# A hybrid decoder step: where the samples' cached keys are turned and multiplied, and how eight PSUM banks are shared out

## The chip, the cores and the metric

The kernel runs on one core of a Trainium2 chip. The metric is the device time of one execution in microseconds (us). A core has TensorE (PE, matrix multiply into PSUM), VectorE (DVE), ScalarE (ACT), GpSimd (POOL) and SyncE (SP), which here issues nearly all DMAs. Each engine works through a list of its own in order; semaphores hold an instruction until what it needs is there. PSUM has eight banks of 512 float32 values in each of 128 partitions.

## The reference

One step of a model with two layers, on a prompt of 2048 tokens and on 8 samples of 4 tokens each, whose past of 2048 tokens lies in a paged cache. The even layer has two branches behind one input projection: a gated recurrence (HGRN2), and "forgetting" attention. The odd layer is a gated recurrence (GLA). What the change touches is the attention of the samples:

```
def fox_sample(q, k, v, log_f, k_pages, v_pages, logf_pages, page_table):
    db, T, H, dh = q.shape                                   # 8, 4, 4, 128
    k_past = k_pages[page_table].reshape(db, -1, H, dh)      # 16 pages of 128 rows for each sample
    v_past = v_pages[page_table].reshape(db, -1, H, dh)
    lf_past = logf_pages[page_table].reshape(db, -1, H)
    suffix_past = (lax.cumsum(lf_past, axis=1, reverse=True) - lf_past).swapaxes(1, 2)
    logit_past = jnp.einsum('bthd,bshd->bhts', q, k_past) * scale + cum_new[..., None] + suffix_past[:, :, None, :]
    ...
    p = jax.nn.softmax(jnp.concatenate([logit_past, logit_new], axis=-1), axis=-1)
    return jnp.einsum('bhts,bshd->bthd', p[..., :P], v_past) + jnp.einsum('bhts,bshd->bthd', p[..., P:], v)
```

The prompt's attention (`fox_prompt`) is causal softmax attention with the same forget bias over the 2048 tokens, 4 heads of 128.

## The kernel before

The kernel has three stages, written one behind the other: `phase_even` (the even layer's projections and its recurrence), `phase_fox` (attention) and `phase_odd` (the even layer's output projection, and the odd layer). A scheduler orders each engine's instructions by their place in the program and by times that it simulates; `issue_after(x)` puts what a block issues behind instruction x on x's engine. Float32 accuracy in the wide matmuls comes from three float16 matmuls (`mm3`, lines 630 to 632).

**The even layer.** The tokens are treated in two halves (hf 0 with the samples' 32 rows, hf 1). Each half has 16 dense units of 256 columns, so units 0 to 15 and 16 to 31 by one count; one unit of the second half is 8 row blocks x 8 k tiles x 3 matmuls. A unit yields after each group of matmuls, in the second half four times (n = 0 to 3). `staged` (line 1267) runs a unit and beside it fetches, measures, scales and splits the weights of units to come; in the second half the split weights are read back from DRAM (`kept_unit`). `mux` lays a head's recurrence (`lin_attn`) beside two or three units. The PSUM banks here are "pj" 3 (projections), "gr" 2 (recurrence, transposes), "st" 1 and "o" 2.

**What runs beside the units.** `beside` (line 1147) loads and measures, from unit 16 on, one after another of the 20 weight units of later layers (`later_unit`; 1 MB each, buffer "lr"), to have their scale ready. `ahead` (line 1537) prepares cached keys. A key group is four pages, one of each of four samples: 1 MB, and there are 32 groups. In 20 units (`AHEAD`) one group is read into `kp` (four DMAs, line 1531), turned by four transposes of 32x32 blocks on DVE into `kt` (`turn_block`, line 1535), and written to the DRAM tensor `kT` (line 1551). Load stands at n = 1, three turns at n = 3, the fourth at n = 0 of the next unit, and the store at its n = 1.

**The attention stage.** `until` (line 97) lays two generators beside each other by costs that are written into their yields. `fox_prompt` works through 16 groups (head, 512 query rows): scores into PSUM banks "s" (2 of them), bias and maximum on DVE (line 1421), exponential on ACT (1429), scaling on POOL (1437), transposes on PE into banks "t" (1457), split on ACT and DVE (1464, 1465), and the product with the values into bank "o". `fox_sample` first goes through the 32 key groups: 20 are read back turned from `kT` (`turned`, line 1591), 12 are read and turned here (`pages`, `turn`). Each group is multiplied with the samples' queries by 16 small matmuls (`score`, line 1697; columns of the array in four strips of 32, `strips` gives them priority over the program's order) into bank "sc". `qz` holds the queries with zeros where a page belongs to another sample. The forget bias (`past`: an indirect gather of log forget values, four transposes, a few matmuls; bank "kt", 2 of them) is added by 64 more small matmuls, then come the softmax, four groups of transposes of the probabilities, and 34 groups of matmuls with the value pages (line 1777).

Of the kernel before, what the change touches and what calls it, by code (L numbers as in the profile page):

```python
# [28 lines left out]
NH = 4  # L29
# [5 lines left out]
SC_C = 1350.0  # L35
# [4 lines left out]
EWR = 3  # L40
# [10 lines left out]
AHEAD = (*range(4, 14), *range(19, 29))  # L51
PRE = len(AHEAD)
TURNED = [n for n in range(2 * 16) if (n + 1) * PRE // 32 > n * PRE // 32]
PAST = 3
VAHEAD = 3
KAHEAD = 6
PKLAG = 4
# [10 lines left out]
PV_C = 5860.0  # L68
# [60 lines left out]
class Kern:  # L129
# [6 lines left out]
    def consts(self):  # L136
# [31 lines left out]
        self.kT = dp.tile([PRE, P, 4 * 512], F32, name="kT")  # L168
# [465 lines left out]
    def proj_fm(self, pps, act, W, off, M, hf, evac, nm):  # L634
        for c0, n in self.segs(hf):
            ps = pps.tile([P, 512], F32, tag="pj", name=f"pf_{nm}{c0}")
            for k in range(KT):
                self.mm3(ps[:M, :n], [x[:, k, off : off + M] for x in W],
                         [x[:, k, c0 : c0 + n] for x in act], k == 0, k == KT - 1)
            evac(ps[:M, :n], c0, n)  # L640
            yield 24 * (n / 2.4 + 3)

    def proj_tm(self, pps, act, W, hf, evac, nm, width=256, pairs=True, banks=("pj",)):
# [3 lines left out]
        for g in range(0, len(tl), per):  # L647
# [8 lines left out]
            for j, (c0, n) in enumerate(grp):  # L656
                for k in range(KT):
                    self.mm3(ps[:n, j], [x[:, k, c0 : c0 + n] for x in act],
                             [x[:, k, :width] for x in W], k == 0, k == KT - 1)
# [463 lines left out]
    def phase_even(self):  # L1123
# [4 lines left out]
        with pool("act", side="right") as ap, pool("w", side="right") as w0, pool("wl", side="right") as wp1, \  # L1128
                pool("wk") as wp0, pool("nrm") as n0, pool("stt") as sp, pool("ps", space=PSUM) as pp0:
            wpool = self.wpool = Pool(w0, {"w": 3, "wr": EWR, "rm": 2, "pow": 2, "lr": 2})  # L1130
            wp = Pool(wp0, {"c4": 7, "sam": 1, "v4": 3, "sg": 3, "pd": 1, "kt": 2, "y": EY, "xpad": 1, "vs": 3,
                            "ss": 2, "rs_t": 2, "rs_r": 2}, Pool(wp1, {"c2": EC2, "th": ETH}))
# [22 lines left out]
            self.later, self.kept = [], {}  # L1155
# [4 lines left out]
            for hf in range(2):  # L1160
# [7 lines left out]
                def dense(a, b, hf=hf):  # L1168
                    return self.staged(us, 16 * hf + a, 16 * hf + b, beside)
# [33 lines left out]
                else:  # L1203
                    self.sx_odd = self.gain_scale(self.g_odd, pps, "pj", "o")
                    self.later = [self.later_unit(wpool, pps, w, cols, key, undo) for w, cols, key, undo in
                                  self.later_units()]
# [7 lines left out]
                drain(dense(2 - hf, 3))  # L1214
                drain(mux(lin(0), LIN_E[hf], dense(3, 5), 2 * cost))
# [35 lines left out]
            for n in range(2):  # L1251
                self.ahead(wpool, 32, n)
# [14 lines left out]
    def staged(self, us, a, b, beside=None):  # L1267
# [15 lines left out]
        for j in range(a, b):  # L1283
# [8 lines left out]
            for n, c in enumerate(us[j][1](self.ready.pop(j))):  # L1292
                for x in todo.pop(0) if todo else ():
                    step(*x)
                if beside:
                    self.ahead(self.wpool, j, n)
                    if n in (1, 3):
                        beside(2 * j + n // 2)
# [54 lines left out]
    def phase_fox(self):  # L1353
# [17 lines left out]
    def fox_prompt(self, fx, pps, caus):  # L1371
# [4 lines left out]
        self.sample_done, self.last_exp, self.pks = False, None, []  # L1376
# [23 lines left out]
        def scores(h, G, b):  # L1400
# [7 lines left out]
            for j in range(G + 1):  # L1408
                w = 512 if j < G else (b + 1) * P
                ps = pps.tile([P, 512], F32, tag="s", name=f"s{h}{tb}{j}")  # L1410
                with ExitStack() as st:
                    if len(self.pks) > PKLAG:
                        st.enter_context(self.tc.issue_after(self.pks[-1 - PKLAG].ins))
                    self.last_pe = self.mm3(ps[:, :w], q, [x[:, :w] for x in K[h, j]], True, True)
# [122 lines left out]
    def ahead(self, pool, u, n):  # L1537
# [3 lines left out]
        m, old = (AHEAD.index(x) if x in AHEAD else None for x in (u, u - 1))  # L1541

        def turns(xs):
            with self.tc.issue_after(self.last_dve.ins):
                for x in xs:
                    self.turn_block(self.kt_ahead, self.kp_ahead, x)

        if n == 0 and old is not None:
            turns([3])
        if n == 1 and old is not None:  # L1550
            nc.sync.dma_start(self.kT[old], self.kt_ahead.rearrange("p a s -> p (a s)"))
        if m is None:
            return
        tag = "lr" if u < 16 else "wr"
        if n == 1:
            self.kp_ahead = pool.tile([P, 4, 512], F32, tag=tag, name=f"kp{m}")
            with self.tc.issue_after(self.last_sp.ins):
                regs = self.page_regs(TURNED[m] % 2, TURNED[m] // 2)
                for x in range(4):
                    self.page_load(self.kp_ahead, "cache_fox_k", regs[x], x)  # L1560
        if n == 3:
            self.kt_ahead = pool.tile([P, NH * 4, P], F32, tag=tag, name=f"kt{m}")
            turns(range(3))

    def fox_sample(self, fs, pps):
# [25 lines left out]
        def turned(n):  # L1591

            kt = fs.tile([P, NH * 4, P], F32, tag="pg", name=f"ktd{n}")
            with ExitStack() as st:
                if len(asked) < 8:
                    st.enter_context(self.tc.issue_after(first_v.ins))
                d = nc.sync.dma_start(kt.rearrange("p a s -> p (a s)"), self.kT[n])
            asked.extend([d] * 4)
            kts.append((kt, [d]))

        yield S0
        marks, steps, first_v = [], [], self.last_vload
# [13 lines left out]
        qz = one([P, 2, NH * 4, TS], "qz")  # L1616
# [672 lines left out]
```

## Time and profile before

| | |
|---|---|
| median of 3 runs | 2319.26 us (2313.12 to 2326.04) |
| the profiled execution | 2321.78 us, its span 2320.1 us |
| mean granted TensorE clock | 0.983 |
| PE busy | 2206.3 us, 95% of the span |
| DVE, ACT, POOL busy | 1399.2, 991.6, 727.1 us |
| DMA | 403.87 MB, mean 174 GB/s |
| even layer, second half | about 480 to 882 us of the span |
| attention stage | about 882 to 1262 us |

A row of the profile's groups names the line, the engine and the operation, what is written from what, the shape and the count; then come the busy time in us and the mean ns of one, then the engine's idle time just ahead of these instructions and who ended it. In tables by stretch each engine has its busy us and its count of instructions; then come the mean granted TensorE clock (1.00 is full), the share of time in which the 16 DMA engines were busy, and GB/s. Rows of instructions in order of time give the start, the length and, in brackets, the idle time ahead and its releaser. PEld is the loading of PE's stationary operand.

### The profile page before, as it was taken

The page shows a single profiled execution, that of the slowest core. Times are in us where ns is not written, and L with a number is a line of the kernel's source. Part 1 is how long each engine was busy: PE and PEld are TensorE (multiplying, and loading weights), DVE is VectorE, ACT ScalarE, POOL GpSimd, SP SyncE. Part 2 cuts the span into 40 slices and gives each one's busy share as a digit, 9 for nine tenths or more (in the row PEclk, how much of TensorE's full clock was granted, in tenths as well). Part 3 has the DMA queues.
Part 4 walks back from the last instruction along what each step waited for, and adds up shares of the span by engine and source line. Part 5 has one row for each costly group of instructions (what it writes and reads, how often), then busy time and mean ns, then how long its engine had stood idle before and what let it go on. Part 6 is the DMA issues. An engine that isn't in the chain of part 4 may idle for free.

```text
span 2320.1 us, 58035 instructions
## 1 busy us (share of the span) xinstructions
PE 2206.3 (95%) x23316; PEld 1580.6 (68%) x23316; DVE 1399.2 (60%) x3138; ACT 991.6 (43%) x2200; POOL 727.1 (31%) x788
## 2 busy tenths in 40 slices
PE   7999999999999996889999999999999999999998
PEld 5677667864655684556446888677677666667887
DVE  7766567626555555768768445366665655547554
ACT  6433344221121223446566443555544545545343
POOL 2223334001111103434346245154452432323232
PEclk9999999999999998999999999999999999999999
DMA  6356665975766549997984969524224431115553
GB/s 203 121 163 187 192 194 188 284 177 172 224 197 183 169 136 271 250 264 271 277 265 142 311 196 262 126 75 146 73 92 97 126 94 58 47 58 165 169 188 151
DMA packets 365296, 403.87 MB, mean 174 GB/s; under 512 B 108529, under 2 KB 303410, under 8 KB 355810
## 3 DMA queue, kind: packets, MB, share of 16 engines
q1 hardware_dynamic: 362882, 393.54, 57.4%
q0 software_dynamic: 2144, 6.62, 0.8%
q8 instruction: 183, 3.00, 0.5%
q14 instruction: 87, 0.71, 0.1%
HBM read 265.77 MB, written 117.39 MB: 165 GB/s over the span
## 4 chain that ended last, share of the span: by engine, by line
PE 69%; DMA 10%; DVE 8%; ACT 4%; issue 4%; SPq 2%; POOL 2%; POOLq 0%; DVEq 0%; ACTq 0%
PE pt_o L630 4%; PE pt_o L631 4%; PE pt_o L632 4%; DMA pgcache_fox_k<-in_cache_fox_k 3%; PE pt_Cv L630 2%; PE pt_Cv L632 2%; PE pt_Cv L631 2%; PE pt L1457 2%; DMA ny<-in_x_prompt 1%; PE pv L1777 1%; PE gl_A L761 1%; PE o_C L914 1%; PE pt_Av L632 1%; PE pt_Av L630 1%; PE pt_Av L631 1%
## 5 line engine op out<-in xcount | busy, mean ns | idle before, releaser
L630 PE MATMUL pt_o<-w_o,act 128*128 128x256 f16 x1024 | 278.9, 273 | 1.3 <-ACT sg1C L687 1.3
L631 PE MATMUL pt_o<-w_o,act 128*128 128x256 f16 x1024 | 278.9, 273 | 0.0
L632 PE MATMUL pt_o<-w_o,act 128*128 128x256 f16 x1024 | 278.7, 273 | 0.0
L630 PEld LDWEIGHTS <-act 128*128 128x128 f16 x2304 | 226.6, 98 | 37.1 <-issue 3.7
L631 PEld LDWEIGHTS <-act 128*128 128x128 f16 x2304 | 226.7, 98 | 33.5 <-issue 4.8
L632 PEld LDWEIGHTS <-act 128*128 128x128 f16 x2304 | 226.6, 98 | 30.7 <-issue 2.2
L794 POOL TENSOR_TENSOR kA<-kA,fA 128x512 f32<-128x512 f32 (+1 forms) x56 | 76.8, 1372 | 338.8 <-PE gl_A L761 275.7
L1429 ACT ACTIVATE L<-L,nm,kc 128x512 f32<-128x512 f32 (+3 forms) x160 | 118.2, 741 | 75.1 <-DVE nm L1427 58.6
L630 PE MATMUL pt_Cv<-w_Cv,act 128*128 128x256 f16 (+1 forms) x512 | 141.4, 276 | 0.3 <-DMA act<-xs 0.3
L632 PE MATMUL pt_Cv<-w_Cv,act 128*128 128x256 f16 (+1 forms) x512 | 141.3, 276 | 0.0
L631 PE MATMUL pt_Cv<-w_Cv,act 128*128 128x256 f16 (+1 forms) x512 | 141.3, 276 | 0.0
L1437 POOL TENSOR_SCALAR L<-L,nm 128x512 f32<-128x512 f32 (+3 forms) x160 | 100.0, 639 | 130.7 <-DVE nm L1433 65.4
L794 POOL TENSOR_TENSOR kC<-kC,fC 128x512 f32<-128x512 f32 (+1 forms) x56 | 81.9, 1463 | 136.3 <-PE gl_C L761 91.4
L1464 ACT ACTIVATE th<-pt 128x512 f16<-128x512 f32 (+3 forms) x159 | 81.0, 527 | 94.6 <-PE pt L1457 92.7
L1465 DVE TENSOR_TENSOR tl<-pt,th 128x512 f16<-128x512 f32 (+3 forms) x159 | 94.5, 605 | 13.0 <-ACT th L1464 11.2
L1457 PE MATMUL pt<-ident,L 128*128 128x128 f32 x544 | 89.6, 280 | 9.4 <-DVE tl L1465 7.5
L1457 PEld LDWEIGHTS pt<-ident,L 128*128 128x128 f32 x544 | 65.5, 143 | 36.1 <-DVE tl L1465 12.8
L793 DVE TENSOR_TENSOR qC<-qC,fC 128x512 f32<-128x512 f32 (+1 forms) x56 | 72.9, 1301 | 21.1 <-PE gl_C L761 21.1
L1977 ACT ACTIVATE vC<-pt_Cv,kc 128x512 f32<-128x512 f32 (+1 forms) x40 | 23.9, 598 | 133.9 <-PE pt_Cv L632 133.9
L630 PE MATMUL s<-k,q 128*128 128x512 f16 (+3 forms) x160 | 57.4, 359 | 20.0 <-DVE mx L1421 16.8
L630 PE MATMUL pt_Bv<-w_Bv,act 128*128 128x260 f16 (+1 forms) x256 | 70.4, 275 | 3.5 <-DVE kc L279 2.3
L630 PE MATMUL pt_Bk<-w_Bk,act 128*128 128x256 f16 x256 | 71.3, 278 | 0.3 <-DVE Bvs L1075 0.3
(961 smaller groups left out, 6473.9 us busy)
## 6 DMA issues: line engine op xcount, KB each, us to landing
pgcache_fox_v<-in_cache_fox_v SPq DMA_DIRECT2D x128, 256.0 KB, 4.5
kp<-in_cache_fox_k SPq DMA_DIRECT2D x80, 256.0 KB, 5.3
kT<-kt SPq DMA_DIRECT2D x20, 1024.0 KB, 5.0
ktd<-kT SPq DMA_DIRECT2D x20, 1024.0 KB, 14.1
yr<-yT SPq DMA_DIRECT2D x16, 1024.0 KB, 7.3
pgcache_fox_k<-in_cache_fox_k SPq DMA_DIRECT2D x48, 256.0 KB, 13.3
x1d<-xo SPq DMA_DIRECT2D x44, 256.0 KB, 4.2
wr_o<-in_w_out_even SPq DMA_DIRECT2D x32, 256.0 KB, 5.5
```

The source lines that it names most:

```text
L630: nc.tensor.matmul(ps, lh[0], rh[0], start=first, stop=False)
L631: nc.tensor.matmul(ps, lh[0], rh[1], start=False, stop=False)
L632: return nc.tensor.matmul(ps, lh[1], rh[0], start=False, stop=last)
L761: nc.tensor.matmul(ps[o : o + M, ch], k[:, ch * P + r : ch * P + r + M], rhs[:, :, 1], start=True, stop=True, tile_position=(0, o))
L793: nc.vector.tensor_tensor(xv[:, :, 1], xv[:, :, 1], t0.to_broadcast([P, nb, w]), ALU.mult)
L794: nc.gpsimd.tensor_tensor(kv[:, :, 0], kv[:, :, 0], t1.to_broadcast([P, nb, w]), ALU.mult)
L1429: self.last_exp = nc.scalar.activation(lt[:, :w], lt[:, :w], AF.Exp, bias=nm[:, 0:1], scale=ib, accum_out=nm[:, 2 + j : 3 + j])
L1437: nc.gpsimd.tensor_scalar(lt[:, :w], lt[:, :w], nm[:, 1:2], 2.0**14, ALU.mult, ALU.mult)
L1457: nc.tensor.transpose(pt[:, w : w + P], rows[b][s // 4][0][:, (s % 4) * P : (s % 4 + 1) * P], self.ident)
L1464: nc.scalar.activation(th[:, a:w], pt[:, a:w], AF.Copy),
L1465: nc.vector.tensor_tensor(tl[:, a:w], pt[:, a:w], th[:, a:w], ALU.subtract)))
L1977: r = nc.scalar.activation(v[h][:, g : g + cnt], ps[:, :, :256], AF.Copy, scale=c)
```

## The change

All 32 key groups are now read, turned and multiplied in the even layer: `KEYS` names steps t = 4 x unit + n, one group in each of the units 13 to 16 and two in each of the units 17 to 30. A group is loaded at step t, two of its turns stand at t+2 and two at t+3, and its 16 matmuls at t+4, in a bank of "gr". The first of two groups of a page number leaves PSUM by a copy on ACT, the second by an addition on DVE, and the sum (128x128) goes to a DRAM tensor `scd` at the next step. `qz` is built in unit 12. `kT` and its stores and reads are gone. The buffers "wr" are four in place of three, "lr" one in place of two. The later weight units are measured in units 4 to 13 and 17 to 26.

In the attention stage the sample reads all finished scores (1 MB) back into `pr`, computes the forget bias into bank "sc", and adds it to the scores on DVE. The costs in the sample's yields are higher (`PV_C` 5860 becomes 10080), so the 34 groups with values are spread over more of the prompt. The banks are now "t" 2, "o" 1, "kt" 1, "s" 3, "sc" 1.

```
-AHEAD = (*range(4, 14), *range(19, 29))
+KEYS = (*range(4 * 13, 4 * 17, 4), *range(4 * 17, 4 * 31, 2))
+LATER = (*range(4, 14), *range(17, 27))
-PV_C = 5860.0
+PV_C = 10080.0
...
-            def beside(x):
-                x -= 33
-                for n in (1, 2):
-                    if 0 <= x - 1 < len(self.later):
-                        self.later[x - 1][n]()
-                if 0 <= x < len(self.later):
-                    self.later[x][0]()
+            def beside(j, n):
+                if n == 0 and j - 1 in LATER:
+                    for step in self.later[LATER.index(j - 1)][1:]:
+                        step()
+                if n == 1 and j in LATER:
+                    self.later[LATER.index(j)][0]()
...
-            pps = Pool(pp0, {"t": 2, "o": 1, "kt": 2}, Pool(pp1, {"s": 2, "sc": 1}))
+            pps = Pool(pp0, {"t": 2, "o": 1, "kt": 1}, Pool(pp1, {"s": 3, "sc": 1}))
...
+    def ahead(self, pool, pps, t):
+        nc, wp = self.nc, self.few
+        if t in (4 * 12, 4 * 12 + 2):
+            self.queries(wp, t % 4)
+        def turns(x):
+            with self.tc.issue_after(self.last_dve.ins):
+                self.made += [self.turn_block(self.kt_ahead, self.kp_ahead, y) for y in (x, x + 1)]
+        if t - 5 in KEYS and KEYS.index(t - 5) % 2:
+            j = KEYS.index(t - 5) // 2
+            nc.sync.dma_start(self.scd[:, j * P : (j + 1) * P], self.scs)
+        if t - 4 in KEYS:
+            j, g = divmod(KEYS.index(t - 4), 2)
+            ps = pps.tile([P, 512], F32, tag="gr", name=f"ks{j}{g}")[:, :P]
+            kt, made = self.kts.pop(0)
+            def score(x, h):
+                return lambda: nc.tensor.matmul(ps[32 * h : 32 * h + 32], self.qz[:, g, 4 * h + x], kt[:, 4 * h + x],
+                                                start=x == 0, stop=x == 3, tile_position=(0, 32 * h))
+            with self.tc.issue_after(self.last_mm.ins):
+                self.strips([score(x, h) for x in range(4) for h in range(NH)], made)
+            if g == 0:
+                self.scs = wp.tile([P, P], F32, tag="scs", name=f"scs{j}")
+                nc.scalar.activation(self.scs, ps, AF.Copy)
+            else:
+                nc.vector.tensor_tensor(self.scs, ps, self.scs, ALU.add)
+        if t - 3 in KEYS:
+            turns(2)
+            self.kts.append((self.kt_ahead, self.made))
+        if t - 2 in KEYS:
+            n = KEYS.index(t - 2)
+            self.kt_ahead, self.made = pool.tile([P, NH * 4, P], F32, tag="wr", name=f"kt{n}"), []
+            self.kp_ahead = self.kps.pop(0)
+            turns(0)
+        if t in KEYS:
+            n = KEYS.index(t)
+            kp = pool.tile([P, 4, 512], F32, tag="wr", name=f"kp{n}")
+            with self.tc.issue_after(self.last_sp.ins):
+                regs = self.page_regs(n % 2, n // 2)
+                for x in range(4):
+                    self.page_load(kp, "cache_fox_k", regs[x], x)
+            self.kps.append(kp)
...
+        nc.sync.dma_start(pr[:, :T], self.scd)
+        yield 8000
...
+        for c in range(4):
+            sc = pps.tile([P, 512], F32, tag="sc", name=f"sc{c}")
+            for jj in range(4):
+                for h in range(NH):
+                    nc.tensor.matmul(sc[32 * h : 32 * h + 32, jj * P : (jj + 1) * P],
+                                     env["sel"][:, 4 * c + jj].rearrange("p b t -> p (b t)"), env["suf"][:, h],
+                                     start=jj == 0, stop=jj == 3, tile_position=(0, 32 * h))
+            part = pr[:, c * 512 : (c + 1) * 512]
+            nc.vector.tensor_tensor_reduce(part, sc, part, 1.0, -3e38 if c == 0 else mx[:, c - 1 : c], ALU.add, ALU.max,
+                                           mx[:, c : c + 1])
```

More of the change, by code (lines that the diff above doesn't have):

```diff
@@ L1168, in dense @@
                 def dense(a, b, hf=hf):
[L1169 removed]
+                    return self.staged(us, 16 * hf + a, 16 * hf + b, beside, pps)
                 lin = lins[hf]
@@ L1214, in phase_even @@
                 drain(dense(2 - hf, 3))
+                if hf == 0:
+                    self.sx_odd = self.gain_scale(self.g_odd, pps, "pj", "o")
+                    self.later = [self.later_unit(wpool, pps, w, cols, key, undo) for w, cols, key, undo in
+                                  self.later_units()]
                 drain(mux(lin(0), LIN_E[hf], dense(3, 5), 2 * cost))
@@ L1250, in phase_even @@
             drain(last)
-            for n in range(2):
-                self.ahead(wpool, 32, n)
+            for t in range(4 * 32, 4 * 32 + 2):
+                self.ahead(wpool, pps, t)
     def later_units(self):
@@ L1294, in staged @@
                     step(*x)
[L1295 to L1298, printed above, removed]
+                if beside and n < 4:
+                    self.ahead(self.wpool, pps, 4 * j + n)
+                    beside(j, n)
                 yield c
@@ L1535, in turn_block, with queries @@
         return self.nc.vector.transpose(kt[:, :, 32 * x : 32 * x + 32], t[:, x].rearrange("p (a e) -> p a e", e=32))
-    def ahead(self, pool, u, n):
+    def queries(self, wp, s):
         nc = self.nc
-        m, old = (AHEAD.index(x) if x in AHEAD else None for x in (u, u - 1))
-        def turns(xs):
-            with self.tc.issue_after(self.last_dve.ins):
[L1545 to L1556, printed above, removed]
+        if s == 0:
+            self.q4 = wp.tile([P, 512], F32, tag="c2", name="q4").rearrange("p (x t) -> p x t", t=TS)
+            self.bm = wp.tile([P, 512], F32, tag="y", name="bm")[:, : 2 * TS].rearrange("p (g c) -> p g c", g=2)
+            self.qz = wp.tile([P, 2, NH * 4, TS], F32, tag="qz", name="qz")
+            for x in range(4):
+                r = slice(32 * x, 32 * x + 32)
+                nc.sync.dma_start(self.q4[r], self.qs.rearrange("h (a e) t -> e (h a) t", e=32))
+                m = self.bm[r].rearrange("p g (b t) -> p g b t", t=DS)
+                nc.gpsimd.memset(m, 1.0)
+                nc.gpsimd.affine_select(m, m, [[-4, 2], [1, DB], [0, DS]], ALU.is_equal, 0.0, base=-x,
+                                        channel_multiplier=0)
+            return
+        with self.tc.issue_after(self.last_dve.ins):
+            for hp in range(2):
+                x = slice(8 * hp, 8 * hp + 8)
+                for g in range(2):
+                    nc.vector.scalar_tensor_tensor(self.qz[:, g, x], self.q4[:, x], self.fsc["q", hp][1],
+                                                   self.bm[:, g : g + 1].to_broadcast([P, 8, TS]), ALU.mult, ALU.mult)
@@ L1589, in pages @@
             return t, r
[L1591 to L1599, printed above, removed]
         yield S0
-        marks, steps, first_v = [], [], self.last_vload
+        marks, first_v = [], self.last_vload
         qs = one([P, NH, TS], "qs")
@@ L1681, in past @@
             nc.vector.reduce_sum(tots, lfp.rearrange("p s h -> p h s"), axis=mybir.AxisListType.X)
-            psf = pps.tile([P, NH, P], F32, tag="kt", name="psf")
+            psf = pps.tile([P, NH, P], F32, tag="sc", name="psf")
             for h in range(NH):
```

114 lines of the change are left out of this document (19 added, 95 removed).

## The prediction

> **What bounds the kernel now.** I read the page's busy shares and 40 slices first, then busy time by stretches, then the waits and single instructions of the stretches that the change touches.
>
> ```profile
> span 2320.1 us, 58035 instructions
> PE 2206.3 (95%) x23316; PEld 1580.6 (68%) x23316; DVE 1399.2 (60%) x3138; ACT 991.6 (43%) x2200; POOL 727.1 (31%) x788
> ...
> PE   7999999999999996889999999999999999999998
> ...
> PEclk9999999999999998999999999999999999999999
> ```
>
> TensorE (PE) is busy for 95% of the span and is the bound, except in slices 16 to 18, where busy time and granted clock dip. Those slices are the start of the attention stage. The busy time by stretch (length, then busy us of PE, PEld, DVE, ACT, POOL, then clock, DMA share, GB/s) shows it:
>
> ```profile
> 480.00:882.00 402.00, 390.78 (x4082) 255.96 (x4080) 213.72 (x490) 84.43 (x215) 54.25 (x57) 0.99 0.60 180
> 882.00:1075.00 193.00, 158.08 (x1798) 102.02 (x1799) 133.81 (x444) 85.35 (x210) 67.74 (x130) 0.90 1.06 273
> 1075.00:1262.00 187.00, 177.90 (x1182) 95.85 (x1180) 142.74 (x465) 118.39 (x279) 86.99 (x140) 0.99 0.69 217
> ...
> 882.00:900.00 18.00, 12.53 (x64) 6.41 (x65) 14.85 (x62) 9.26 (x25) 7.44 (x15) 0.91 1.04 252
> 1100.00:1220.00 120.00, 116.03 (x762) 56.44 (x761) 84.04 (x280) 70.23 (x170) 48.87 (x86) 0.99 0.87 273
> 1220.00:1262.00 42.00, 38.15 (x264) 25.32 (x264) 36.53 (x101) 29.45 (x66) 24.61 (x31) 1.00 0.21 70
> ```
>
> The even layer's second half, where the change puts the keys (480 to 882), leaves PE only 11.2 us idle: what is added to PE there is paid in full. From 882 to 1075 the DMA engines are full (share 1.06), PE is idle for 34.9 us and its mean clock is 0.90. That is where cached keys are read, turned on VectorE (DVE) and multiplied beside the prompt. From 1100 to 1220, with only cached values to read, PE is at 96.7% (116.03 of 120).
>
> ```profile
> pgcache_fox_k<-in_cache_fox_k SPq DMA_DIRECT2D x48, 256.0 KB, 13.3
> ktd<-kT SPq DMA_DIRECT2D x20, 1024.0 KB, 14.1
> kT<-kt SPq DMA_DIRECT2D x20, 1024.0 KB, 5.0
> L1535 DVE STREAM_TRANSPOSE kts<-pgcache_fox_k 128x512 f32<-128x512 f32 x48 | 32.1, 694 | 28.0 <-DMA pgcache_fox_k<-in_cache_fox_k 26.3 <-issue 1.7
> ...
> L1681 DVE TENSOR_REDUCE tots<-lfp 128x4 f32<-128x512 f32 x1 | 1.1, 1068 | 5.5 <-DMA lfp<-in_cache_fox_logf,pcol 5.5
> ...
> PE s L630 <- DVE mx L1421: 14.6, 7, 7.5
> PE pt L1457 <- DVE tl L1465: 6.7, 4, 3.7
> PE sc L1697 <- DMA ktd<-kT: 6.1, 2, 4.6
> ```
>
> DVE stands idle 26.3 us for key pages, in order, so the prompt's scores behind it are not taken out of PSUM; PE then waits 14.6 us for DVE to free a score bank (the three last rows: waits of PE from 882 to 1075, total, times, longest).
>
> **The change, part by part.** *Taken out of the attention stage:* 48 page loads of 256 KB, 20 reads of 1 MB, 48 turns on DVE (32.1 us), the building of the zeroed queries on DVE, and the key multiplications on PE:
>
> ```profile
> L1697 PE MATMUL sc<-ktd,qz 128*32 128x128 f32 x640 | 22.9, 295 | 6.1 <-DMA ktd<-kT 6.1
> L1697 PE MATMUL sc<-kts,qz 128*32 128x128 f32 x384 | 15.5, 312 | 1.0 <-DVE kts L1535 1.0
> ...
> L1630 DVE SCALAR_TENSOR_TENSOR qz<-q,kc 128x256 f32<-128x256 f32 x4 | 1.8, 478 | 0.0
> ```
>
> Without these 38.4 us of PE, 158.08 - 38.4 = 119.7 us are left to 1075, at clock 0.90; at the 0.99 of the stretch behind they would be 108.8. With that stretch's 177.9 the stage needs 286.7 us of PE. DVE needs 276.5 (133.8 + 142.7) - 32.1 - 1.8 = 242.6 us. At 96.7% PE takes 296.5 us. Two losses stay: the first 18 us, where PE does 12.53 us of work because the short first rows are bound by DVE (14.85 of 18), cost 5; and DVE's wait of 5.5 us for the gathered log forget values, so far beside waits for pages, may now show: I take half, 2.5, between 0 and 5.5. That makes 304 us, with DVE at 242.6/304 = 80%. The stretches say what DVE's load costs PE: at 70% of DVE (84.04 of 120) PE runs at 96.7%, at 87% (36.53 of 42) at 90.8%. On a line between them 80% gives 93.2%, 307.6 + 7.5 = 315 us. Before it was 380 (882 to 1262): 65 us saved. Ends: 76 at 96.7%, and 54 at 90.8% with the whole 5.5.
>
> The third score bank, the loss of the second bank for turned tiles and the wider costs of the sample's steps only order this work. From 1075 on, PE waited 2.2 us for score banks:
>
> ```profile
> PE s L630 <- DVE mx L1421: 2.2, 5, 0.6
> ```
>
> so the third bank's worth is in the pace already taken; I add nothing (0 to -2). One bank for four transposes in a row puts an ACT copy between them: 0 to +3, taken 0, since prompt work lies between the sample's steps. The value pages keep their number; spread over more of the stage they ask for less than the 273 GB/s that 1100 to 1220 carried at 96.7% of PE. The one read of 1 MB of finished scores replaces 32 MB.
>
> *Put into the even layer:* 32 groups of 16 small matmuls. In these rows each appears as 32 instructions:
>
> ```profile
> 942.00 0.38 PE L632 MATMUL s<-k,q 128*128 128x512 f16 x1
> 942.31 1.08 PE L1697 MATMUL sc<-ktd,qz 128*32 128x128 f32 x32
> 943.32 0.49 PE L1688 MATMUL psf<-stri,lfTs 128*128 128x128 f32 x2
> ...
> 951.45 1.08 PE L1697 MATMUL sc<-kts,qz 128*32 128x128 f32 x32
> 952.35 1.06 PE L1697 MATMUL sc<-ktd,qz 128*32 128x128 f32 x32
> ```
>
> One alone holds PE for 1.01 us from start to start, and 0.1 more is lost ahead of it (the matmul at 942.00 would have let the next start near 942.2): 1.11. Directly behind another group a group takes 0.90. In the even layer each stands alone among wide matmuls: 32 x 1.11 = 35.5 us, all on the path, as PE has no idle time there. Ends: 28.8 (0.90 each), and 62 at the 1.94 of a group at half clock:
>
> ```profile
> 912.31 0.61 PE L630 MATMUL s<-k,q 128*128 128x512 f16 x1 [7.54 <-DVE mx L1421]
> 912.71 0.63 PE L631 MATMUL s<-k,q 128*128 128x512 f16 x1
> ...
> 914.13 1.94 PE L1697 MATMUL sc<-kts,qz 128*32 128x128 f32 x32
> ```
>
> After a wait of 7.54 us PE runs at half speed for some microseconds. The Trainium skill ("TensorE: Matmul & The Clock Gate", Part 1) puts this down to an activity window of about 3.4 us, idle longer than which halves the clock. The trace agrees; by that rule shorter waits would leave the groups at 1.11. The Trainium skill ("TensorEngine Tiling (Array Packing)", Key Properties) also says that a change of tiling mode drains PE, which speaks against scattering the groups. The rows above price it at 1.11 - 0.90 = 0.21 us a group, 6.7 us in all; without it the sum would be better by that.
>
> A new wait stands on PE: a group starts only when four turns of its page are done. Behind it the layer's matmuls stand, and DVE and ACT, which empty them. The cover is the distance in the program: load at step t, turns at t+2 and t+3, group at t+4, a step being a quarter of a unit (402/16 = 25 us). The load must itself wait, on SP's queue, for the group of step t to leave its buffer; stores and weight loads stand behind it there, some 1 us, hidden by the two units that weights are fetched ahead. What a late page does is on record:
>
> ```profile
> 772.33 1.24 SPq L1551 DMA_DIRECT2D kT<-kt  x1
> ...
> 778.33 1.37 SPq L1531 DMA_DIRECT2D kp<-in_cache_fox_k  x3
> ...
> 786.41 1.90 DVE L1535 STREAM_TRANSPOSE kt<-kp 128x512 f32<-128x512 f32 x3 [8.00 <-DMA kp<-in_cache_fox_k]
> ...
> PE gl_A L761 <- DVE qA L793: 4.1, 1, 4.1
> ```
>
> A load came late behind the store of a turned page, DVE stood 8.00 us and PE 4.1, the one such stall among ten pages of this half. The stores go, the pages triple: -4.1 to +12 (three stalls), taken 0. The groups also take one of two PSUM banks that the recurrence uses. The wait of 2.2 us in 5 times, 0.44 each, on a like bank would make 14 for 32 groups; with evictions of a 128x128 tile it is nearer to 0: +2.
>
> DVE in this half:
>
> ```profile
> L1535 DVE STREAM_TRANSPOSE kt<-kp 128x512 f32<-128x512 f32 x40 | 25.9, 685 | 9.8 <-DMA kp<-in_cache_fox_k 9.7
> L307 DVE TENSOR_REDUCE rm_o<-lr_o 128x1 f32<-128x512 f32 x24 | 14.7, 672 | 0.0
> ```
>
> 128 turns of 0.685 replace 40 (+62 us), ten weight units' reductions (40 x 0.672 = 27 us) move to the first half, where as many us of turns leave. 213.7 + 35 is 57% of DVE, hidden behind PE. The DMA moves about the same there: ten stores and ten weight units of 1 MB go, some 20 key pages and 1 MB of scores come, at share 0.60. In the first half 20 MB of keys go and 10 of weights come: 0 for PE. The queries' loads and masks move to the last unit before, off PE: 0.
>
> Sum: -65 + 35.5 + 0 + 2 = -27.5. The profiled execution took 2321.78 (span 2320.1 and 1.7 around it) and would take 2294; it is 2.5 above the median of the three runs, 2319.26. Against that I forecast **2292**.
>
> **The rivals.** *More gain.* PE keeps 96.7% through the stage and the 4.1 us stall goes with the stores: -76 + 35.5 - 4.1 = -45, 2275. For it: that pace was held for 120 us at full clock with the prompt under way. Against it: the values that filled PE there are spread thinner.
>
> *No change: VectorE becomes the stage's bound.* From 882 to 900 DVE at 82% left PE only 70%. If PE falls to 85%, the stage takes 286.7/0.85 + 7.5 = 345 us, 35 saved, and the groups eat it: 2321. Against it: 90.8% of PE beside 87% of DVE behind 1220.
>
> *Slower: each group waits on PE for its page's last turn.* It decides at 65/32 = 2.0 us a group. With 1.00 us of waiting, as before the first group of the old stage (the idle of 1.0 in the row of kts), and half clock, 2.94 x 32 = 94: +29, 2348. For it: DVE is in order and waits up to 8.00 us there. Against it: the old turns of this half, at the same distance from their loads, cost PE one stall. By the clock rule of the Trainium skill cited above the groups would stay at 1.11 behind waits of 1.00, and this rival would end at -65 + 32 x 2.11 = +2.5, 2322.
>
> **How the numbers follow.** The forecast 0.56 (its own range 2278 to 2307), more gain 0.17, no change 0.14, slower 0.13. Half a per cent, 11.6 us, is about what a measurement of this kernel can tell from no change; so faster 0.73, same 0.14, slower 0.13. The range 2262 to 2326 goes from the gain's far end (-76, and 28.8 for the groups, less 4.1 for the stall: some -51, with a little for the runs' spread) to the no-change case with as much, and leaves out the slower case and a little below.
>
> **What would show it.** Right: the attention stage about 315 us, no half clock in it, DMA share there below 0.9; 32 groups of about 1.1 us in the even layer's second half, which gets longer by 35 to 40; PE's waits there for turns (kt) or pages few. Wrong: PE idle ahead of the groups or of the recurrence's matmuls by more than 1 us each, clock dips before 900, or DVE near 90% beside PE at 85% in the attention stage.

## The result and the profile after

The changed kernel takes 2302.81 us (median of 4 runs, 2301.61 to 2304.24) where the kernel before, in the same rounds, takes 2319.45 (4 runs, 2313.12 to 2326.04): a ratio of 0.9928, 95% interval 0.9900 to 0.9957. Forecast were 2292 us, in a range from 2262 to 2326. It is 0.7% faster, by 16.6 us where 27 were forecast: the time is 10.8 us over the forecast.

The page of the changed kernel, its busy shares and slices:

```profile
span 2302.6 us, 58047 instructions
PE 2203.6 (96%) x23316; PEld 1573.8 (68%) x23316; DVE 1398.7 (61%) x3154; ACT 994.1 (43%) x2216; POOL 723.8 (31%) x787
...
PE   7999999999999999899998999999999999999998
...
PEclk9999999999999999899999999999999999999999
```

PE's busy time is 2.7 us less than before, so nearly the whole gain is idle time closed. The dip of three slices at the start of the stage has become a dip of one (slice 17, 921 to 979); slice 22, at the stage's end, is another in the busy time.

I cut both kernels at the same events: the first matmul of Bv's unit 0 (`pt_Bv`; unit 13, still in the even layer's first half, where the changed kernel reads its first key group), the first score matmul of the prompt (`s`) and the first matmul of the odd stage (`pt_o`). Before they stand at 393.1, 882.9 and 1268.5, after at 393.6, 917.5 and 1252.3. From these: even layer from unit 13 to its end (called units 13 to 31 below) 489.8 to 523.9 (+34.1), attention stage 385.6 to 334.8 (-50.8), odd stage 1051.6 to 1050.3 (-1.3). Busy time by stretch, after:

```profile
393.60:917.50 523.90, 504.39 (x5857) 348.96 (x5855) 297.12 (x628) 116.07 (x297) 57.99 (x54) 0.99 0.66 175
917.50:1252.30 334.80, 306.06 (x2015) 174.90 (x2016) 254.28 (x866) 207.88 (x503) 161.79 (x277) 0.96 0.64 192
917.50:937.50 20.00, 16.20 (x69) 8.17 (x69) 13.12 (x64) 8.95 (x25) 10.06 (x25) 0.68 1.08 298
```

and before, by the same bounds:

```profile
393.10:882.90 489.80, 471.90 (x4843) 326.50 (x4841) 273.44 (x621) 110.09 (x277) 62.00 (x64) 0.99 0.66 193
882.90:1268.50 385.60, 342.49 (x3039) 203.83 (x3040) 280.89 (x915) 208.13 (x495) 158.20 (x273) 0.95 0.88 246
```

In the stage the DMA share fell from 0.88 to 0.64 and PE's idle time from 43.1 to 28.7 us (length less busy time), but its clock only rose from 0.95 to 0.96: the row from 917.50 to 937.50 shows 20 us at a mean of 0.68. In units 13 to 31 PE's busy time grew by 32.5 us and its idle time by 1.6.

The waits of PE in the stage after (total, times, longest):

```profile
PE fo L625 <- ACT th L1455: 9.5, 10, 2.0
PE pt L1448 <- DVE tl L1456: 5.9, 13, 1.0
...
PE s L625 <- DVE mx L1412: 2.4, 4, 1.3
```

and before, by the same bounds:

```profile
PE s L630 <- DVE mx L1421: 16.8, 12, 7.5
PE pt L1457 <- DVE tl L1465: 7.5, 7, 3.7
...
PE fo L631 <- DVE tl L1465: 5.4, 7, 2.3
```

The waits for score banks (`mx`) are down from 16.8 us to 2.4. The waits for ACT and DVE to split turned tiles (`th`, `tl`) stay, and are now the longest: 16.1 us, with 0.7 in a row that is not shown, where they were 14.3, with 1.4 in such a row.

PE's waits in units 13 to 31, and one group of key matmuls in its place:

```profile
PE ks L1571 <- DVE scs L1580: 3.0, 1, 3.0
...
PE ks L1571 <- DVE kt L1526: 1.0, 2, 0.6
```

```profile
909.07 0.27 PE L626 MATMUL pt_Bv<-w_Bv,act 128*128 128x256 f16 x1
909.27 1.08 PE L1571 MATMUL ks<-kt,qz 128*32 128x128 f32 x32
910.28 0.28 PE L627 MATMUL pt_Bv<-w_Bv,act 128*128 128x256 f16 x1
```

PE waits for a turned page twice, 1.0 us in all. A group holds PE from 909.18 (0.11 after the matmul ahead of it, at the pace of its neighbours) to 910.28, 1.10 us, as forecast.

### The profile page after: what moved, and what is told of

The parts are those of the page before. It is cut to its first block, busy times and chain, and to the rows that moved or that the text cites. A ratio compares the mean times of both kernels' runs of the same rounds, so it can differ in the third digit from the quotient of the medians.

```text
span 2302.6 us, 58047 instructions
## 1 busy us (share of the span) xinstructions
PE 2203.6 (96%) x23316; PEld 1573.8 (68%) x23316; DVE 1398.7 (61%) x3154; ACT 994.1 (43%) x2216; POOL 723.8 (31%) x787
## 4 chain that ended last, share of the span: by engine, by line
PE 40%; DVE 3%; ACT 3%; POOL 2%; DMA 2%; issue 1%; SPq 0%; POOLq 0%; DVEq 0%; ACTq 0%
PE pt_o L626 4%; PE pt_o L625 4%; PE pt_o L627 4%; PE pt_Cv L625 2%; PE pt_Cv L627 2%; PE pt_Cv L626 2%; PE o_C L909 1%; PE gl_C L756 1%; DMA yr<-yT 1%; PE pt L1448 1%; POOL s_C L842 1%; PE py_C L728 1%; ACT L L1420 1%; DMA wr_o<-in_w_out_odd 1%; PE pv L1750 0%
## 5 line engine op out<-in xcount | busy, mean ns | idle before, releaser
L627 PEld LDWEIGHTS <-act 128*128 128x128 f16 x2304 | 226.2, 98 | 32.5 <-issue 3.7
L1526 DVE STREAM_TRANSPOSE kt<-kp 128x512 f32<-128x512 f32 x128 | 82.1, 684 | 41.2 <-DMA kp<-in_cache_fox_k 40.2
L1448 PEld LDWEIGHTS pt<-ident,L 128*128 128x128 f32 x544 | 67.0, 145 | 43.1 <-DVE tl L1456 17.5
L1950 ACT ACTIVATE vC<-pt_Cv,kc 128x512 f32<-128x512 f32 (+1 forms) x40 | 23.9, 599 | 133.8 <-PE pt_Cv L627 133.7
L625 PE MATMUL fo<-th,v 128*128 128x512 f16 (+3 forms) x174 | 59.9, 344 | 13.2 <-ACT th L1455 9.5
```

The source lines that it names most:

```text
L625: nc.tensor.matmul(ps, lh[0], rh[0], start=first, stop=False)
L627: return nc.tensor.matmul(ps, lh[1], rh[0], start=False, stop=last)
L1448: nc.tensor.transpose(pt[:, w : w + P], rows[b][s // 4][0][:, (s % 4) * P : (s % 4 + 1) * P], self.ident)
L1526: return self.nc.vector.transpose(kt[:, :, 32 * x : 32 * x + 32], t[:, x].rearrange("p (a e) -> p a e", e=32))
L1950: r = nc.scalar.activation(v[h][:, g : g + cnt], ps[:, :, :256], AF.Copy, scale=c)
```

## The experiments

Theory: the gain is PE's own time, freed in the stage by the multiplications and by the DMA, less what the groups cost in the even layer; the stage falls short of the forecast by the waits for turned tiles and the clock. Rivals: the reads alone did it; DVE's turns did it; the banks did it.

| run | time (us) | ratio to before, 95% | units 13 to 31 | stage |
|---|---|---|---|---|
| changed, again | 2302.34 | 0.9926 (0.9904 to 0.9948) | 524.4 | 332.6 |
| old banks | 2302.47 | 0.9922 (0.9900 to 0.9945) | 523.6 | 327.5 |
| turned tiles 3, scores 2 | 2294.89 | 0.9890 (0.9868 to 0.9913) | 522.1 | 326.9 |
| shared banks | 2292.53 | 0.9884 (0.9861 to 0.9906) | 523.3 | 321.4 |
| no key work | 2248.96 | 0.9693 (0.9630 to 0.9757) | 475.5 | 328.2 |
| a quarter of the matmuls | 2280.49 | 0.9829 (0.9765 to 0.9893) | 505.2 | 329.7 |
| prompt's cost 465000 | 2297.87 | 0.9897 (0.9869 to 0.9924) | 522.6 | 323.4 |
| before, keys read once | 2293.31 | 0.9879 (0.9847 to 0.9910) | 487.1 | 358.8 |
| ... and turned once | 2293.99 | 0.9878 (0.9841 to 0.9915) | 489.6 | 361.5 |
| ... and a quarter of the matmuls | 2271.14 | 0.9782 (0.9750 to 0.9813) | 487.9 | 337.2 |
| shared banks, cost 465000 | 2300.24 | 0.9915 (0.9890 to 0.9940) | 523.8 | 327.1 |
| ... and three tiles ahead | 2292.92 | 0.9887 (0.9861 to 0.9914) | 523.0 | 321.0 |

The kernel before took 2321.03 beside the first four, 2321.23 beside the next four and 2322.61 beside the last four. "No key work" and the first "a quarter of the matmuls" rest on two executions each, the others on four to nine.

The two columns at the right come from one profiled execution of each kernel, and that one can lie off its kernel's median: 9.3 us below it for the old banks (2293.21), 7.0 below for the cost of 465000 (2290.89), 4.8 above for the keys read once (2298.07). The changed kernel's two profiles differ by 2.2 us in the stage (334.8, 332.6), and the old banks' stage is 5 to 7 us shorter at the same median time. So a difference of less than some 7 us between two stages shows nothing by itself. The lengths of units 13 to 31 are steadier: 522.1 to 524.4 in the eight profiles with the whole key work there.

**The changed kernel again.**

> The changed kernel again, as the base for the runs beside it. It was 2302.8 us against 2319.5 before (ratio 0.9928); its attention stage, from the first score matmul at 917.5 to the first output-projection matmul at 1252.3 us, took 334.8 us against 385.6. Both theories expect the same again: 2300 to 2306.

2302.34 us (2297.69 to 2306.54), the mark for the three runs that follow.

**The banks as before.**

```
-            pps = Pool(pp0, {"t": 2, "o": 1, "kt": 1}, Pool(pp1, {"s": 3, "sc": 1}))
+            pps = Pool(pp0, {"t": 2, "o": 1, "kt": 2}, Pool(pp1, {"s": 2, "sc": 1}))
```

> The changed kernel with the PSUM banks of the attention stage as before: two for the prompt's scores, two for kt. Theory (the gain is the freed DMA and the moved multiplications; the banks only order the work): within 4 us of the changed kernel, 2300 to 2308. Rival (the third score bank carries a part of the gain): at least 8 us slower than the changed kernel, 2311 or more, with PE's waits for score banks (s behind DVE's mx), 2.4 us in the changed kernel, back above 8.

2302.47 us: the third score bank brings nothing that can be measured. With it gone PE waits for score banks 6.2 us in 13 times, and less for `th` (4.1).

**The bank to the turned tiles.**

```
+            pps = Pool(pp0, {"t": 3, "o": 1, "kt": 1}, Pool(pp1, {"s": 2, "sc": 1}))
```

> The changed kernel with the third bank given to the prompt's turned tiles (t 3, s 2, kt 1). In the changed kernel's stage PE waits 16 us in sum for the split of turned tiles (9.5 for ACT's th, 6.6 for DVE's tl) and 2.4 for score banks. Theory A (these waits are for a bank, and are most of what the stage takes beyond the forecast): 4 to 10 us faster than the changed kernel, 2293 to 2299. Theory B (they are latency of the split itself, with work behind it in order): within 3 us, 2300 to 2306. If the score banks were what helped: slower by 4 or more.

2294.89 us (2289.84 to 2297.79), 7.5 less than the changed kernel in the same rounds.

**Three and three, the sample's transposes in the prompt's banks.**

```
+            pps = Pool(pp0, {"t": 3, "o": 1}, Pool(pp1, {"s": 3, "sc": 1}))
-                pt = pps.tile([P, 512], F32, tag="kt", name=f"lfT{h}")
+                pt = pps.tile([P, 512], F32, tag="t", name=f"lfT{h}")
... (and so the other tiles of tag "kt" in this pool)
```

> The changed kernel with the bank kt given up: its users (forget bias, turned probabilities, turned outputs) share three banks t with the prompt's turned tiles; scores keep three. Theory A of the run before: 4 to 10 us faster than the changed kernel, 2293 to 2299. Theory B: within 3 us of it. A third way: the sample's tiles hold prompt banks for as long as DVE and ACT take to empty them, and it is slower by 3 or more.

2292.53 us (2289.26 to 2296.92), 9.8 less, the lowest time of all versions that do the whole work (the last one below, at 2292.92, is as good). Four of PE's waits in its stage, and its middle 200 us, the changed kernel's row behind it:

```profile
PE ppt L1725 <- DVE pr L1717: 4.2, 1, 4.2
PE fo L626 <- DVE tl L1456: 3.5, 10, 0.8
PE fo L625 <- ACT th L1455: 3.4, 5, 1.3
PE s L625 <- DVE mx L1412: 3.3, 5, 1.1
```

```profile
1000.00:1200.00 200.00, 196.68 (x1290) 110.31 (x1288) 160.20 (x545) 136.88 (x337) 94.20 (x168) 1.00 0.66 203
```

```profile
1000.00:1200.00 200.00, 188.57 (x1193) 101.81 (x1194) 150.45 (x501) 124.99 (x303) 86.74 (x155) 0.98 0.68 204
```

Waits for the split of turned tiles fall from 16.1 us to 6.9, and PE runs at 98.3% in place of 94.3% in those 200 us. So the bank that the change gave to the scores was wanted by the turned tiles. Not all of it is gained: a wait for the sample's probabilities (`pr`) comes up, and PE's idle time in the whole stage falls by 6.1 us (28.7 to 22.6). PE's busy time differs by 7.3 us between these two profiles (306.06 and 298.80), which the waits do not explain.

**No key work in the even layer.** Reads, turns and matmuls are left out, and zeros are stored as scores.

```
-                self.strips([score(x, h) for x in range(4) for h in range(NH)], made)
-                nc.scalar.activation(self.scs, ps, AF.Copy)
+                nc.vector.memset(self.scs, 0.0)
... (page loads and turns out)
```

> The changed kernel without the keys' work in the even layer: no page is read, turned or multiplied there, and zeros are stored as scores (one small memset for two groups); the rest is as it was. The even layer's second half began its attention stage at 917.5 us in the changed kernel and at 882.9 before, where 10 of the groups were still read and turned in it. Theory (a group costs what PE needs for it, 1.1 us, and its reads and turns are hidden): the stage begins 32 to 39 us earlier, at 879 to 886, and the whole is 2264 to 2271. Rival (reads, turns and waits cost PE something of their own): earlier by 45 or more, 2258 or less.

Units 13 to 31 take 475.5 us: 48.4 less than in the changed kernel, so the rival's number came. From 510 on PE is hardly ever idle:

```profile
510.00:868.00 358.00, 356.76 (x3872) 231.15 (x3870) 156.86 (x340) 78.11 (x203) 50.40 (x48) 1.00 0.32 102
```

PE is idle for 1.2 us from 510 on, where the changed kernel is idle for 8.8 (395.21 busy of 404, from 510 to 914). In the whole of units 13 to 31 PE's busy time differs by 36.3 us (504.39 and 468.12) and its idle time by 12.1 (19.5 and 7.4); of these 3.0 is the wait just ahead of the stage, which here comes behind the first three score matmuls (2.82 us), so inside the stage. The kernel before, too, takes longer than this one there, by 489.8 - 475.5 = 14.3 us, 10.5 of them idle time of PE: it turns twelve groups there (48 turns) and stores them, and it measures 20 later weight units where the other two kernels measure ten. How much of the 14.3 us each of the two costs was not measured. The difference, 48.4 - 14.3, is the +34.1. Its stage, 328.2, is 4.4 and 6.6 us shorter than in the two profiles of the changed kernel, which by itself shows nothing; more on that below.

**A quarter of the matmuls.** Of a group's 16 only the 4 of one x are left, reads and turns stay.

```
-                self.strips([score(x, h) for x in range(4) for h in range(NH)], made)
+                self.strips([score(x, h) for x in range(1) for h in range(NH)], made)
```

> The changed kernel with 4 of the 16 matmuls of each key group (the first of the four blocks), all reads and turns as they were. If the price is PE's own time, some 0.9 us for 32 instructions and 0.2 for the change of tiling, three quarters of 0.9 x 32 = 22 us go: 2279 to 2284. If the price is mostly what surrounds a group (waiting, draining), under 10 us go: 2293 or more.

2280.49 us, units 13 to 31 at 505.2: 18.7 us less for three quarters of the matmuls, 0.58 us a group. PE's busy time there fell by 21.2 (504.39 to 483.20), its idle time rose by 2.5. PE's own time sets the cost; it is not spread evenly, since a whole group holds 1.10 us and the 4 matmuls that stay still take some 0.5 of it.

**The prompt's cost in the merge at 465000.**

```
-FOX_S = 500000.0
+FOX_S = 465000.0
```

> The changed kernel with the sample spread over more of the prompt (500000 becomes 465000 in the ratio of the two): its last value matmul was at 1198 us, 54 us before the end of the stage, and PE is busy for 18.4 of 20 us and less there. Theory (values fill PE's gaps; a stage with an even spread is better): 2 to 6 us faster than the changed kernel. Rival (the gaps are as long anywhere, and the tail in which the output projection is prepared gets shorter): within 2, or slower.

2297.87 us over 9 runs that spread from 2288.07 to 2304.96: the interval overlaps the changed kernel's, so 4.5 us of gain is not settled.

**The kernel before, its keys read once in the stage.** One turned group and one page group are read and used for all, so the scores are of wrong keys; turns and matmuls stay, 31 MB of reads go.

```
+            if "kt" not in once:
+                kt = fs.tile([P, NH * 4, P], F32, tag="ktd1", name="ktd1")
+                ...
+            kts.append(once["kt"])
...
-                    yield from turn(pages("cache_fox_k", g, j)[0], g, j)
+                    if "pg" not in once:
+                        once["pg"] = pages("cache_fox_k", g, j)[0]
+                    yield from turn(once["pg"], g, j)
```

> The kernel before, with its attention stage reading one turned group and one unturned group of pages once and using them again and again: 31 MB of reads are left out there (the scores are of the wrong pages); the turns on DVE and all multiplications stay in the stage, page buffers are one fewer. Theory (the old stage lost 35 us of PE idle time and some 13 to a lower clock because DVE and PE waited for pages): 2319 falls by 30 to 48, 2271 to 2289, and the clock from 900 to 1075 us rises from 0.90 to 0.97 or more. Rival (the reads were hidden, and the change gained by moving DVE's turns and PE's multiplications out of a stage that DVE's own order holds up): it falls by less than 15.

2293.31 us, the stage 358.8, 26.8 less than before:

```profile
880.20:1239.00 358.80, 332.35 (x3039) 197.91 (x3040) 280.79 (x915) 208.41 (x495) 159.13 (x273) 0.98 0.59 176
...
900.00:1075.00 175.00, 165.41 (x1953) 107.64 (x1957) 146.61 (x489) 100.60 (x239) 77.64 (x144) 1.00 0.43 128
```

The same 3039 matmuls take 10.1 us less (342.49 to 332.35) at a clock of 0.98, and 16.7 us of idle time go. The reads alone were worth more than half of the stage's gain. By the medians the kernel falls by 27.9 us, just short of the 30 to 48 of the theory and well over the rival's 15.

**And turned once.**

```
-                    yield from turn(once["pg"], g, j)
+                        yield from turn(once["pg"], g, j)
+                    else:
+                        kts.append(once["kt"])
+                        yield 4 * SC_C
```

> The kernel before with key groups read once in the attention stage, as in the run before it, and now also turned once there: 44 of the 48 turns on DVE (30 us) are left out, the products use a group that is there already, so their values are not the reference's. All 32 groups are still multiplied on PE. The kernel with the reads alone left out took 2293.3 us, its stage 358.8 us (880.2 to 1239.0). Moving the whole of the key work out of the stage (the changed kernel) gave 334.8 us, that is another 24 for 33.9 us of DVE and 38.4 us of PE. Theory (PE is the stage's bound once the reads are gone, so the 24 are PE's own multiplications): the stage loses 0 to 8 us, 351 to 359, the time 2285 to 2294. Rival (DVE's turns are what delays the scores): the stage loses 15 to 25 us, 334 to 344, the time 2268 to 2278, and PE's waits for DVE mx (11.4 us in the run before) fall to 4 or less.

2293.99 us, the stage 361.5: DVE's 44 turns cost nothing that can be measured. The wait for `mx` did fall, though not to the rival's 4 us, and waits for value pages grew in its place. The two waits, in the run with the turns and in the one without:

```profile
PE s L630 <- DVE mx L1421: 11.5, 14, 3.9
...
PE pv L1778 <- DMA pgcache_fox_v<-in_cache_fox_v: 2.7, 1, 2.7
```

```profile
PE pv L1781 <- DMA pgcache_fox_v<-in_cache_fox_v: 6.4, 3, 3.3
PE s L630 <- DVE mx L1421: 5.6, 11, 2.9
```

**And a quarter of the matmuls.**

```
-            self.pks.append(self.strips([score(h, g, j, x, kt, sc) for x in range(4) for h in range(NH)],
+            self.pks.append(self.strips([score(h, g, j, x, kt, sc) for x in range(1) for h in range(NH)],
```

> As the run with groups read and turned once, and of the 16 matmuls of a group only the 4 of one index x are left: 384 of 512 matmuls, 28.8 us of PE's 38.4 us, go out of the attention stage, so the scores are not the reference's. Theory (PE's own time): the stage is 20 to 29 us shorter than in that run, near 330 to 338. Rival (the multiplications lie in gaps that PE has anyway, and DVE's turns carried the 24 us): 0 to 10 us shorter than in that run.

2271.14 us, 22.9 less than with all of them, the stage 337.2, 24.3 less. The stage without turns, then with a quarter of the matmuls:

```profile
884.40:1245.90 361.50, 334.26 (x3040) 202.39 (x3041) 256.37 (x871) 206.97 (x495) 157.66 (x273) 0.97 0.58 175
```

```profile
881.30:1218.50 337.20, 310.33 (x2272) 178.88 (x2273) 256.25 (x871) 206.19 (x495) 157.82 (x273) 0.98 0.63 187
```

Busy time falls by 23.9, and idle time stays (27.2 and 26.9). Scaled to all 16 matmuls, the 32 groups are 24.3 x 16/12 = 32.4 us, 1.01 a group; by the medians 22.9 x 16/12 = 30.5. That the 4 that stay cost just their quarter is an assumption here.

**The two gains together.** The shared banks, and `FOX_S` at 465000.

> The changed kernel with three banks for turned tiles, shared with the sample's transposes, beside three for scores (2292.5 us, 9.8 less than the changed kernel), and now also the cost of the prompt in the merge with the sample at 465000 in place of 500000, which alone brought 4.5 us at a wide spread. Theory (separate gaps: one takes PE's waits for turned tiles away, the other fills the prompt's end): 2285 to 2290. Rival (both close the same gaps at the end of the stage): 2291 to 2295.

2300.24 us, 7.7 more than the shared banks alone had in their rounds. Neither expectation came. Its list of waits has one that the other lacks, at the stage's end:

```profile
PE pt_o L625 <- ACT act L1853: 5.8, 1, 5.8
```

**And three turned tiles ahead.**

```
-            ahead = [turn(j) for j in range(min(2, nj))]
+            ahead = [turn(j) for j in range(min(3, nj))]
```

> As the run with shared banks and the prompt's cost at 465000, and three turned tiles are made ahead of the product with the values in place of two, as there are three banks for them. Theory (PE still waits for ACT and DVE to split a turned tile, 6.9 us in 15 times with the shared banks): these waits fall to 2 us or less, 3 to 6 us off. Rival (a third tile ahead only moves the wait to the transposes, which need a bank that the split has freed): no change within 2 us.

2292.92 us, 7.3 less than without, but no better than the shared banks alone. The waits for `th` and `tl` are 5.2 us in 11 times here and 7.0 in 13 there, and the wait of 5.8 us is gone; which of the two moved the time is not settled.

## Why the prediction was right, and by how much it was off

**The even layer: +34.1 against +37.5 (35.5 for the groups, 2 for the banks).** Right in the net and in the price of a group (1.10 us in place, 1.11 forecast). DVE waited for pages far more than before:

```profile
DVE kt L1526 <- DMA kp<-in_cache_fox_k: 40.2, 10, 18.8
```

In the kernel before it was 9.7 us in 2 times (both from 480 on). The forecast took the price of late pages to PE at 0, between -4.1 and +12, and as a difference that held: PE's idle time from 510 to just before the stage is 8.8 us after and 9.2 before. But without key work it is 1.2, so some 8 us are paid in both kernels. The sum had no term for that, nor for the 14.3 us that the kernel before loses there to its own groups and weight units; that the two cancel to within 2 us of idle time (+1.6) is luck. Key work costs 48.4 us there, not 37, and 14.3 were paid already. The slower rival asked for a wait of 1.00 us ahead of each group; there were two for turned pages, 1.0 us in all. The bank term, forecast at 2, was one wait of 3.0 us for the sum (`scs`).

**The attention stage: -50.8 against -65. Here the step failed, in two terms.** The clean way to read it is by busy and idle time. By these bounds my sum was 342.49 - 38.4 - 10.9 (clock) = 293.2 us of PE and 28.3 idle (315 - 286.7). After it is 306.06 and 28.7: the idle time was right, PE's work was 12.9 us more.

First, the multiplications were taken out at 38.4 us, the sum of their rows, and put in at 1.11 a group, a hold from start to start. A row lasts longer than it holds PE (1.08 us, with the next start after 1.01 or 0.90), and the 38.4 also has groups at half clock in it (the row of 1.94 us). Measured (a quarter of the matmuls, in the kernel before with reads and turns once) and scaled, 32 groups are 32.4 us, or 30.5 by the medians: 6.0 to 7.9 too much, from an inconsistency that the rows of the prediction show (1.01 and 0.90 a group, against 38.4/32 = 1.20).

Second, the clock. That it recovers when the reads go is right: 10.1 us less for the same matmuls with the keys read once, 10.9 forecast. But the changed kernel loses it again at the stage's start. "No half clock in it" was wrong:

```profile
917.52 0.26 PE L625 MATMUL s<-k,q 128*128 128x128 f16 x1 [3.03 <-DVE Bvs L1070]
917.59 0.31 PE L626 MATMUL s<-k,q 128*128 128x128 f16 x1
...
920.94 0.59 PE L625 MATMUL s<-k,q 128*128 128x512 f16 x1 [1.33 <-DVE mx L1412]
...
929.15 0.63 PE L627 MATMUL s<-k,q 128*128 128x512 f16 x1
...
930.86 0.38 PE L626 MATMUL s<-k,q 128*128 128x512 f16 x1
```

Matmuls of 512 columns last 0.63 us until 930, and 0.38 from there: 12.7 us of half clock. The kernel before begins the stage with the same idle time, and is slow for 3.3 us (883.74 to 887.02):

```profile
882.90 0.22 PE L630 MATMUL s<-k,q 128*128 128x128 f16 x1 [3.03 <-DMA vn<-vs]
...
883.74 0.46 PE L630 MATMUL s<-k,q 128*128 128x384 f16 x1 [0.18 <-DVE mx L1421]
...
886.59 0.63 PE L631 MATMUL s<-k,q 128*128 128x512 f16 x1
887.02 0.48 PE L632 MATMUL s<-k,q 128*128 128x512 f16 x1
```

The difference begins with the wait of 1.33 us at 920.94. DVE, named there, was itself waiting for POOL, and POOL for the bias row:

```profile
920.58 0.29 DVE L1412 CUSTOM_DVE_ANT_0 L<-s,cm 128x128 f32<-128x128 f32 x1 [3.16 <-POOL cm L1398]
```

```profile
920.10 1.31 POOL L1398 TENSOR_TENSOR cm<-cb,caus 128x128 f32<-128x128 f32 x3 [3.80 <-DMA cb<-cbd]
```

And the bias row was asked for late, on SP's queue:

```profile
899.50 6.72 SPq L1084 DMA_DIRECT2D vd<-Bvs  x2
910.74 0.34 SPq L1564 DMA_DIRECT2D scd<-scs  x1
911.17 0.41 SPq L1084 DMA_DIRECT2D vd<-Bvs  x1
911.67 1.71 SPq L1384 DMA_DIRECT2D q<-qd  x1
...
914.87 0.51 SPq L1377 DMA_DIRECT2D cb<-cbd  x1
```

```profile
SPq L1564 <- DVE scs L1580: 4.7, 2, 4.4
```

The last key group is multiplied at 909, and SP waits for its sum to store it (`scd`, 4.4 us). The prompt's first loads (`q`, `k`, `cb`) stand behind this store, and behind three stores of Bv's results (`vd`). They go out 5.9 us ahead of the first score matmul; before, 19.8 us ahead, and there the stores of Bv's results stand behind them:

```profile
863.12 0.56 SPq L1390 DMA_DIRECT2D q<-qd  x1
...
865.88 0.47 SPq L1383 DMA_DIRECT2D cb<-cbd  x1
...
868.28 0.53 SPq L1089 DMA_DIRECT2D vd<-Bvs  x1
```

The wait for the sum alone does not make the loads late. The store of Bv's results at 911.17, the last thing ahead of them, needs what DVE finishes at 911.09, so in this order they would have gone out no sooner:

```profile
910.62 0.47 DVE L1070 SCALAR_TENSOR_TENSOR Bvs<-pt_Bv,kc,Bvs 128x256 f16<-128x256 f32 x1
```

What differs is their place on the queue. Why the scheduler puts them there when the key groups stand in the program up to the end of the layer was not looked into. Without key work the loads go out 16.6 us ahead, and the first 20 us of the stage run at 0.91 in place of 0.68:

```profile
868.10:888.10 20.00, 13.04 (x71) 6.81 (x68) 17.10 (x76) 12.19 (x31) 10.81 (x26) 0.91 1.06 271
```

The other runs fit. In all nine profiles with key matmuls in the even layer the loads go out 5.5 to 5.9 us ahead, and the first 20 us run at 0.66 to 0.83; in the kernel before, its three variants and the kernel without key work they go out 16.6 to 19.8 us ahead, and these 20 us run at 0.84 to 0.91. A version that moves the loads alone, or ends the key groups a step or two earlier, which would show the cause by itself, was not run. The prediction did look at what stands behind a waiting transfer on SP's queue, but behind the page loads and not at the start of the next stage.

The price of the half clock is an estimate. PE was busy for 16.20 of those 20 us; at the 0.99 of the forecast the same work takes 16.20 x 0.68/0.99 = 11.1, so some 5 us were lost. With the 6.0 to 7.9 of the multiplications that is 11 to 13 of the 12.9 us. In the changed kernel's second profile, with the same start (0.67), PE's work in the stage is 302.73 us, so the sum is short by 9.5 there; the two terms are known to a few us and no better. Put together from the runs: 385.6 - 26.8 (reads) + 2.7 (turns, which is within the noise) - 32.4 (matmuls) = 329.1, and the changed kernel's stage without key work is 328.2.

**The pace by DVE's load: the number right by luck.** I set PE's pace by a line through DVE's load. With the turns and without them (DVE at 280.79/358.8 = 78% and 256.37/361.5 = 71%) PE's idle time is 26.5 and 27.2 us. So DVE's load did not set it over this range, and the rival in which DVE becomes the bound found no support. The largest part of the 28.7 us of idle time, 16.1, are the waits for turned tiles, for which the sum had no term of its own; a third bank for them took 9.2 of these away in the run with shared banks. They lie inside the forecast idle time, so they are not what the stage fell short by, as the theory ahead of the runs had it.

**The banks: 0 forecast for the third score bank, 0 measured** (2302.34 and 2302.47).

**The rule on the clock.** Idle times of 3.03 us halved the clock here, within 0.1 us after the change and 0.8 us before it; in the kernel without key work one of 2.82 us did, within 0.6 us. The Trainium skill ("TensorE: Matmul & The Clock Gate", Part 1), which the prediction cited, gives about 3.4 us of idleness for that, so less than its figure was enough. The trace of the kernel before had such a case in its first key group, at half clock (1.94 us at 901.47) behind idle times of 2.79 and 1.00 us.

## What to carry to other kernels

Price a group of small instructions the same way where it leaves and where it comes in: by its hold from start to start, not by the sum of its rows. When work is moved to the end of a stage, look at its last piece, and at where the next stage's first loads end up on the queue: ahead of that piece's stores or behind them. Before a buffer is given to the longest wait, ask which wait comes up when that one goes; here the same bank was worth 0 us with the scores and 7.5 with the turned tiles.

## What was not expected of the hardware

The half clock outlasts its cause. After the same 3.03 us of idleness it held for 3.3 us before the change and for 12.7 after it. After the change the work was broken by idle times of 1.33, 0.37 and 0.73 us, and full speed came 4.8 us into the first stretch without any (925.47 to 930.22). In the kernel without key work, where nothing broke the work, it held for 3.4 us (871.75 to 875.2); with the bank at the turned tiles, where one wait of 2.85 us did, for 6.8 (the mean clock of its first 20 us is 0.83, and 0.17 x 20 us at half clock is twice as long). So a short wait while the clock is halved seems to cost more than its length; no run takes one such wait away and nothing else. The Trainium skill (the same page and Part) says that the clock comes back after about 3.4 us of sustained activity; 3.3, 3.4 and 4.8 us agree with it roughly.
